# Narrower last key tile and first score block, a shorter inverse square root, and a final scaling in quarters

## The chip, the cores and the metric

The kernel runs on one core of one Trainium2 chip. The metric is the device time of one execution in microseconds (us), the median of several runs. Engines go by the names of the profile: PE is TensorE (PEld its weight loads), DVE is VectorE, ACT is ScalarE, POOL is GpSimd, SP is the engine that issues most DMAs.

## What is computed

One layer on 1024 tokens of width 1024, in float32: an RMS norm, one input projection, latent attention with 16 heads, a gated output projection added to x, then a second gated product (the embedding part, called PLE), and a final RMS norm. What matters here is the attention of one query block of 128 tokens, which sees only the keys up to its own end:

```python
for blk in range(S // Q_BLOCK):          # 8 blocks of 128 queries
    q0, q1 = blk * Q_BLOCK, (blk + 1) * Q_BLOCK
    s = (q_nope[q0:q1] @ k_nope[:q1].T + q_rope[q0:q1] @ k_rope[:q1].T) * scale
    s = where(k_chunk <= q_chunk, s, -inf)      # chunks of 64 tokens
    outs.append(softmax(s) @ v[:, :q1])
...
return rmsnorm(x, final_norm)            # x * (mean(x*x) + eps) ** -0.5 * gain
```

## The kernel before

Every matrix operand is split into a high part and the rest (`hi`, `lo`, both of type float32r), and a product is made of three matmuls, hi by hi, hi by lo and lo by hi. Each matmul of the program comes with a load of its own stationary operand of 128x128.

The work goes in stages: the projection of the norms (`u_tile`, with L215 and L216), the gate path (L513), the attention over 16 heads, the output projection and the PLE product (both in `product`, L751).

In the attention, `blocks` (L683) lists 16 heads times 8 query blocks, in the order 5, 4, 2, 3, 7, 6, 0, 1 within a head (the last head has its own order). One loop (L685) runs over them with an offset for each step: `scores` for block n, `prob_transposes` for block n-2, `values` for block n-4. The projections of later heads are put between them (L690 to L706). That program order is PE's order.

- `scores` (L598) multiplies one query block with its keys, three matmuls for each span of columns. Block 0 has 128 keys; its span is 256 columns wide (L604), of which `s` (L611) uses the first 128. The masking, the maximum and the exponential follow on DVE and ACT.
- `prob_transposes` (L641) transposes the probabilities tile by tile on PE into a PSUM tile; ACT copies them out as `hi` (L650) and DVE subtracts to get `lo` (L651). Two query blocks of a pair g = i // 2 share one tile: the even block is in columns 0 to 127, the odd one in columns 128 to 255.
- `values` (L653) multiplies the values with the pair's probabilities, 2g + 2 key tiles, a `hi` and a `lo` matmul for each, 256 columns wide. The even block does not see the last key tile, so its half of that tile is zero; four memsets (L537 to L539) set these zeros once.

At the end, each token tile goes through the PLE product, a sigmoid, two elementwise operations and a sum of squares; `rsqrt` (L93) makes the inverse root on DVE with an integer estimate and three Newton steps, and the tile is scaled and stored (L838 to L845). For the last tile, POOL has multiplied columns 0 to 511 with the gain beforehand (L836), and ACT scales them while DVE scales and multiplies the others. The two halves are then stored by two DMAs from SP. `rsqrt` is also called for the norms of `u_tile` (two columns), once for eight columns (L381), and for each of the 16 tiles of the two last stages (one column).

Of the kernel before, what the change touches and what calls it, by code (L numbers as in the profile page):

```python
# [9 lines left out]
F32 = mybir.dt.float32  # L10
F32R = mybir.dt.float32r
BF16 = mybir.dt.bfloat16
I32 = mybir.dt.int32
AF = mybir.ActivationFunctionType
ALU = mybir.AluOpType
AX = mybir.AxisListType

P = 128
S = 1024
D = 1024  # L20
# [31 lines left out]
def mla_ple_kernel(ctx, tc, x, x_t, p_t, pos, norm_g, w_c, w_z, q_norm, w_q, w_r, kv_norm, w_k, w_v,  # L52
# [6 lines left out]
    nc = tc.nc  # L59
    V, A, G = nc.vector, nc.scalar, nc.gpsimd  # L60

    def pool(name, bufs=1, **kw):
        return tc.tile_pool(name=name, bufs=bufs, **kw)
# [3 lines left out]
    def ps_big():  # L67
        return psum.tile([P, 1024], F32, tag="big", name="ps_big", bufs=2)

    def ps_tr():  # L70
        return psum.tile([P, 512], F32, tag="one", name="ps_tr", bufs=4)

    def ps_o():
        return psum.tile([P, 512], F32, tag="one", name="ps_o", bufs=4)

    def ps_pj():
        return psum.tile([P, 512], F32, tag="one", name="ps_pj", bufs=4)
# [10 lines left out]
    small = ctx.enter_context(pool("small", bufs=4))  # L88
# [3 lines left out]

    def rsqrt(v, n, name="rs_y", bufs=None):  # L93

        half = small.tile([P, n], I32, tag=f"rs_i{n}", name="rs_i", bufs=2)
        V.tensor_scalar(out=half, in0=v.bitcast(I32), scalar1=1, scalar2=None,
                        op0=ALU.logical_shift_right)
        y = small.tile([P, n], F32, tag=f"{name}{n}", name=name, bufs=bufs)
        V.tensor_scalar(out=y.bitcast(I32), in0=half, scalar1=-1, scalar2=0x5F3759DF,
                        op0=ALU.mult, op1=ALU.add)  # L100
        t = small.tile([P, n], F32, tag=f"rs_t{n}", name="rs_t", bufs=2)
        if n == 1:
            h = small.tile([P, 1], F32, tag="rs_h", name="rs_h", bufs=2)
            V.tensor_scalar(out=h, in0=v, scalar1=-0.5, scalar2=None, op0=ALU.mult)
            for _ in range(3):
                V.tensor_scalar(out=t, in0=y, scalar1=y, scalar2=h, op0=ALU.mult, op1=ALU.mult)
                V.scalar_tensor_tensor(out=y, in0=t, scalar=1.5, in1=y, op0=ALU.add, op1=ALU.mult)
            return y
        for _ in range(3):
            V.scalar_tensor_tensor(out=t, in0=y, scalar=-0.5, in1=y, op0=ALU.mult, op1=ALU.mult)  # L110
            V.tensor_tensor(out=t, in0=t, in1=v, op=ALU.mult)
            V.scalar_tensor_tensor(out=y, in0=t, scalar=1.5, in1=y, op0=ALU.add, op1=ALU.mult)
        return y
# [37 lines left out]
    ps = ps_tr()  # L151
# [232 lines left out]
    for t in range(NT):  # L384
        V.tensor_scalar(out=krw[:, t, :], in0=krw[:, t, :], scalar1=rx[:, t:t + 1], scalar2=None,
                        op0=ALU.mult)
# [116 lines left out]
    for c in range(KT):  # L503
        ps = ps_big()
        for k in range(KT):
            if k % 4 == 0:
                n = 2 * c + k // 4
# [3 lines left out]
            for a, b in pairs:  # L511
                for hf in range(2):
                    nc.tensor.matmul(ps[:, hf * 512:(hf + 1) * 512], wz[b][:, k % 4, :],  # L513
                                     (hT_hi, hT_lo)[a][:, k, hf * 512:(hf + 1) * 512],
                                     start=k == 0 and a + b == 0, stop=k == KT - 1 and a == 1)
# [18 lines left out]


    pt_w = [[att.tile([P, n, 2 * P], F32R, name=f"pt{n}{z}") for z in "hl"] for n in (4, 8)]
    for n, w in zip((4, 8), pt_w):  # L537
        for z in w:
            G.memset(z[:, n - 1, :P].bitcast(F32), 0.0)  # L539
    pt = [[z[:, (2, 0, 2, 0)[g]:, :] for z in pt_w[g // 2]] for g in range(4)]  # L540
    vals = att.tile([P, NT, 2, 4, VD], F32R, name="vals")
    kst = att.tile([P, S], F32, name="kst")

    def prob_tile():
        return att.tile([P, S], F32, tag="prob", name="prob", bufs=3)
# [49 lines left out]
    def order(h):  # L595
        return LAST if h == H - 1 else ORDER

    def scores(h, i):  # L598
        e = h % 2
        q = q_of[h]  # L600
        qs = slice(i * P, (i + 1) * P)
        n = (i + 1) * P
        off = P if n == 640 else 0
        spans = {128: [(0, 256)], 640: [(0, 384), (384, 640)]}.get(  # L604
            n, [(a, min(a + 512, n)) for a in range(0, n, 512)])
        ps = ps_big() if n > P else ps_tr()
        for s0, s1 in spans:
            for a, b in pairs:
                nc.tensor.matmul(ps[:, off + s0:off + s1], q[a][:, qs], (k_hi, k_lo)[b][e][:, s0:s1],  # L609
                                 start=a + b == 0, stop=a == 1)  # L610
        s = ps[:, off:off + n]  # L611
        V.memset(s[0:64, n - 64:], MASKED)
        mx = small.tile([P, 1], F32, tag="mx", name="mx")
        V.tensor_reduce(out=mx, in_=s, axis=AX.X, op=ALU.max, negate=True)  # L614
        pr = prob_tile()
        if e == 0 and i == order(h)[0]:
            sums[h // 2] = small.tile([P, 2 * NT], F32, tag="l", name="l", bufs=2)
        l = sums[h // 2][:, e * NT + i:e * NT + i + 1]
        A.activation(out=pr[:, :n], in_=s, func=AF.Exp, bias=mx, scale=1.0, accum_out=l)  # L619
        return pr  # L620
# [32 lines left out]
    def values(h, g):  # L653
        e, c = h % 2, h // 2
        hi, lo = pt[g]
        ps = ps_o()
        last = 2 * g + 1
        for j in range(last + 1):
            w = vals[:, j, c % 2, 2 * e:2 * e + 2, :]
            for n, z in enumerate((hi, lo)):  # L660
                nc.tensor.matmul(ps[:, :256], w, z[:, j, :], start=j + n == 0, stop=j == last and n == 1)  # L661
        top, bot = slice(e * VD, (e + 1) * VD), slice((1 - e) * VD, (2 - e) * VD)
        o = att.tile([P, 256], F32, tag="o1", name="o1", bufs=2)
        A.copy(out=o[top], in_=ps[bot, :256])
        V.tensor_tensor(out=o[top], in0=ps[top, :256], in1=o[top], op=ALU.add)  # L665
        z = zT[top, c, g * 256:(g + 1) * 256]
        (V if h >= H - 2 else G).tensor_tensor(out=z, in0=o[top], in1=z, op=ALU.mult)  # L667
# [17 lines left out]
    for n in range(len(blocks) + LAGV):  # L685
        if n < len(blocks):
            h, i = blocks[n]
# [21 lines left out]
        if n >= LAGV and (blocks[n - LAGV][1] ^ 1) in order(blocks[n - LAGV][0])[:(n - LAGV) % NT]:  # L709
            h, i = blocks[n - LAGV]  # L710
# [34 lines left out]
    halves = (slice(0, 512), slice(512, D))  # L745

    def product(ps, st, w, nk, spans):
        for k in range(nk):
            for a, b in pairs:
                for o, cols in zip(ps, spans):  # L750
                    nc.tensor.matmul(o, st[a][:, k, :], w[k][b][:, cols],  # L751
                                     start=k == 0 and a + b == 0, stop=k == nk - 1 and a == 1)
# [9 lines left out]
    xs = fin.tile([P, NT, D], F32, name="xs")  # L762
# [26 lines left out]
    for t in range(NT):  # L789
# [4 lines left out]
        ps = ps_big()  # L794
# [17 lines left out]
    for t in range(NT):  # L812
        (gl, pl), nxt = nxt, gate_lhs(t + 1) if t + 1 < NT else None
        ps = ps_big()
        last = t == NT - 1
        edges = (0, 512, 768, D) if last else (0, 512, D)
        spans = [slice(*z) for z in zip(edges, edges[1:])]
        pp = [ps_pj()[:, :z.stop - z.start] for z in spans]
        ms = small.tile([P, 3], F32, tag="ms2", name="ms2", bufs=2)
        for i, cols in enumerate(spans):  # L820
            n = cols.stop - cols.start
            po = ps_tr()[:, :n] if i == 2 else ps[:, cols]
            product([po], gl, w_g, KT, [cols])
            if i != 1:
                product(pp[i:i + 2], pl, w_p, PLE // P, spans[i:i + 2])
            sg = fin.tile([P, 512], F32, tag="sg", name="sg", bufs=2)[:, :n]
            A.activation(out=sg, in_=po, func=AF.Sigmoid, scale=r2[t])
            V.tensor_tensor(out=sg, in0=pp[i], in1=sg, op=ALU.mult)
            V.tensor_tensor(out=xs[:, t, cols], in0=xs[:, t, cols], in1=sg, op=ALU.add)  # L829
            jk = fin.tile([P, D], BF16, tag="jk", name="jk", bufs=1)  # L830
            mean_square(ms[:, i:i + 1], xs[:, t, cols], D, jk[:, :n])
            if i:
                V.scalar_tensor_tensor(out=ms[:, i:i + 1], in0=ms[:, i - 1:i], scalar=EPS if i == 1 else 0.0,
                                       in1=ms[:, i:i + 1], op0=ALU.add, op1=ALU.add)
            elif last:
                G.tensor_tensor(out=xs[:, t, cols], in0=xs[:, t, cols], in1=f_bc[:, cols], op=ALU.mult)  # L836
        r = rsqrt(ms[:, i:i + 1], 1, name="r3", bufs=2)
        for hf in range(2):  # L838
            cols = halves[hf]
            if last and hf == 0:  # L840
                A.activation(out=xs[:, t, cols], in_=xs[:, t, cols], func=AF.Copy, scale=r)
            else:
                V.scalar_tensor_tensor(out=xs[:, t, cols], in0=xs[:, t, cols], scalar=r,
                                       in1=f_bc[:, cols], op0=ALU.mult, op1=ALU.mult)
            nc.sync.dma_start(out=out[t * P:(t + 1) * P, cols], in_=xs[:, t, cols])  # L845


# [48 lines left out]
```

## Time and profile before

| | |
|---|---|
| median of 3 runs | 719.05 us (718.22 to 720.75) |
| profiled execution | 719.65 us, span 717.9 us |
| PE busy | 703.2 us (98%), 4032 matmuls |
| PEld busy | 612.9 us (85%), 4032 loads |
| DVE busy | 523.8 us (73%) |
| ACT busy | 400.5 us (56%) |
| POOL busy | 214.2 us (30%) |
| TensorE clock granted | full in nearly all of the span (mean 0.998) |

The span is the stretch that the profile covers; the execution's own time is 1.75 us more. Matmuls are pipelined and their ends are modelled, so a busy PE is not a PE at its peak: what one matmul costs in a dense stream is the distance from its start to the next start, not its duration.

### The profile page before, as it was taken

Reading aid. Unit: us, or ns where it says so; the run is one execution under the profiler, and the core shown is the slowest. Engines: PE = TensorE matmul, PEld = TensorE weight load, DVE = VectorE, ACT = ScalarE, POOL = GpSimd, SP = SyncE. Lnnn points to the kernel's source line nnn. Section 1 sums busy time; section 2 is a strip of 40 time slices with the busy share of each in tenths; the row PEclk is TensorE's granted clock in tenths of the full one; section 3 lists DMA queues with packets and bytes.
Section 4 is the critical chain, followed back from the end, with each engine's and each line's share of the span. In section 5 each row is a group of like instructions: output and inputs, shape, how many; then the busy total and the mean of one; then the engine's idle time right before and its main releaser. Section 6 shows DMA issues by size and latency. Waiting matters only on the chain.

```text
span 717.9 us, 11582 instructions
## 1 busy us (share of the span) xinstructions
PE 703.2 (98%) x4032; PEld 612.9 (85%) x4032; DVE 523.8 (73%) x1298; ACT 400.5 (56%) x920; POOL 214.2 (30%) x236
## 2 busy tenths in 40 slices
PE   9999999999999999999999999989999999999995
PEld 7999888888988899889988899878878888888884
DVE  6995553417888888888888888899564168888754
ACT  6752343417777767877767787776353145342322
POOL 0000443214145434554335532264155142000000
PEclk9999999999999999999999999999999999999999
DMA  8720334314103402052211421032573030111101
GB/s 318 279 89 12 122 100 125 103 60 110 38 16 108 147 31 74 1 181 74 66 40 60 136 60 60 15 108 85 179 265 115 1 102 24 38 37 37 60 30 59
DMA packets 26907, 63.95 MB, mean 89 GB/s; under 512 B 4568, under 2 KB 8544, under 8 KB 26848
## 3 DMA queue, kind: packets, MB, share of 16 engines
q1 hardware_dynamic: 23168, 52.19, 22.8%
q0 software_dynamic: 3536, 11.02, 4.6%
q8 instruction: 32, 0.52, 0.3%
q14 instruction: 27, 0.22, 0.1%
q10 hardware_dynamic: 144, 0.00, 0.0%
HBM read 50.01 MB, written 13.18 MB: 88 GB/s over the span
## 4 chain that ended last, share of the span: by engine, by line
PE 90%; DVE 3%; ACT 3%; DMA 2%; issue 1%; POOL 0%; SPq 0%; ACTq 0%; DVEq 0%
PE ps_big L751 21%; PE ps_big L609 13%; PE ps_big L513 12%; PE ps_o L661 10%; PE ps_tr L121 9%; PE ps_pj L423 6%; PE ps_big L215 4%; PE ps_pj L751 3%; PE ps_pj L570 3%; PE ps_pj L553 3%; PE ps_big L216 3%; PE ps_o L215 1%; PE ps_pj L216 1%; DMA wst<-in_w_out 1%; ACT prob L619 1%; PE ps_tr L609 1%
## 5 line engine op out<-in xcount | busy, mean ns | idle before, releaser
L751 PE MATMUL ps_big<-w,aTh 128*128 128x512 f32 (+1 forms) x480 | 139.0, 390 | 0.0
L751 PEld LDWEIGHTS ps_big<-w,aTh 128*128 128x128 f32 x480 | 89.4, 188 | 20.2
L619 ACT ACTIVATE prob<-ps_big,mx 128x384 f32<-128x384 f32 (+6 forms) x112 | 89.4, 798 | 16.2 <-DVE mx L614 15.5
L614 DVE TENSOR_REDUCE mx<-ps_big 128x1 f32<-128x384 f32 (+6 forms) x112 | 91.6, 818 | 1.8
L121 PE MATMUL ps_tr<-ident,prob 128*128 128x128 f32 x576 | 84.1, 273 | 2.0 <-ACT prob L619 2.0
L751 PE MATMUL ps_big<-w,aTl 128*128 128x512 f32 (+1 forms) x240 | 84.6, 390 | 0.0
L121 PEld LDWEIGHTS ps_tr<-ident,prob 128*128 128x128 f32 x576 | 68.3, 140 | 11.7 <-ACT prob L619 2.8
L91 DVE TENSOR_TENSOR pt8l<-ps_tr,pt8h 128x512 fp32r<-128x512 f32 (+3 forms) x128 | 71.0, 582 | 4.5 <-ACT pt8h L650 3.8
L667 POOL TENSOR_TENSOR zT<-o,zT 64x256 f32<-64x256 f32 x56 | 41.1, 736 | 94.2 <-DVE o L665 80.6
L609 PE MATMUL ps_big<-k_hi,qh 128*128 128x512 f32 (+2 forms) x176 | 67.7, 385 | 0.9 <-ACT prob L619 0.8
L650 ACT CAST pt8h<-ps_tr 128x512 fp32r<-128x512 f32 (+3 forms) x128 | 60.7, 509 | 4.7 <-PE ps_tr L121 4.3
L609 PE MATMUL ps_big<-k_lo,qh 128*128 128x512 f32 (+2 forms) x176 | 62.0, 352 | 0.0
L609 PE MATMUL ps_big<-k_hi,ql 128*128 128x512 f32 (+2 forms) x176 | 61.4, 349 | 0.0
L661 PE MATMUL ps_o<-pt8h,vals 128*128 128x256 f32 x224 | 57.6, 294 | 0.0
L661 PE MATMUL ps_o<-pt8l,vals 128*128 128x256 f32 x224 | 55.0, 282 | 0.0
L751 PEld LDWEIGHTS ps_big<-w,aTl 128*128 128x128 f32 x240 | 45.0, 188 | 10.2 <-POOL aTl L91 0.5
L116 ACT ACTIVATE jk<-xs 128x512 bf16<-128x512 f32 (+2 forms) x25 | 18.8, 751 | 45.2 <-DVE xs L829 37.3
L661 PEld LDWEIGHTS ps_o<-pt8l,vals 128*128 128x128 f32 x224 | 42.9, 191 | 0.0
L661 PEld LDWEIGHTS ps_o<-pt8h,vals 128*128 128x128 f32 x224 | 42.6, 190 | 0.0
L650 ACT CAST pt4h<-ps_tr 128x384 fp32r<-128x384 f32 (+3 forms) x64 | 27.2, 426 | 27.3 <-PE ps_tr L121 27.1
L360 ACT ACTIVATE zh<-zs,g_col 128x128 fp32r<-128x128 f32 x56 | 18.3, 392 | 42.1 <-DMA zs<-in_w_z 36.1
L609 PEld LDWEIGHTS ps_big<-k_hi,qh 128*128 128x128 f32 x176 | 33.2, 189 | 7.7 <-ACT prob L619 3.5
(285 smaller groups left out, 1740.2 us busy)
## 6 DMA issues: line engine op xcount, KB each, us to landing
zT<-in_x SPq DMA_DIRECT2D x8, 512.0 KB, 5.0
rlb<-rl SPq DMA_DIRECT2D x32, 128.0 KB, 3.1
wst<-in_w_out SPq DMA_DIRECT2D x8, 512.0 KB, 4.4
xs<-in_x SPq DMA_DIRECT2D x8, 512.0 KB, 7.2
wst<-in_ple_gate SPq DMA_DIRECT2D x8, 512.0 KB, 4.0
out<-xs SPq DMA_DIRECT2D x16, 256.0 KB, 2.0
zs<-in_w_z SPq DMA_DIRECT2D x14, 256.0 KB, 2.9
zT<-in_x_t SPq DMA_DIRECT2D x6, 512.0 KB, 4.1
```

The costliest lines, as they stand in the source:

```text
L91: eng.tensor_tensor(out=lo, in0=src, in1=hi.bitcast(F32), op=ALU.subtract)
L121: nc.tensor.transpose(dst[:, j * P:(j + 1) * P], src[:, j * P:(j + 1) * P], ident)
L215: nc.tensor.matmul(pq, st, mv[:, k, :QL], start=first, stop=last)
L423: nc.tensor.matmul(ps, w[b][:, k, :], (cq_hi, cq_lo)[a][:, k, hf * 512:hf * 512 + 512], start=k == 0 and a + b == 0, stop=k == n - 1 and a ...
L513: nc.tensor.matmul(ps[:, hf * 512:(hf + 1) * 512], wz[b][:, k % 4, :], (hT_hi, hT_lo)[a][:, k, hf * 512:(hf + 1) * 512], start=k == 0 and ...
L609: nc.tensor.matmul(ps[:, off + s0:off + s1], q[a][:, qs], (k_hi, k_lo)[b][e][:, s0:s1], start=a + b == 0, stop=a == 1)
L614: V.tensor_reduce(out=mx, in_=s, axis=AX.X, op=ALU.max, negate=True)
L619: A.activation(out=pr[:, :n], in_=s, func=AF.Exp, bias=mx, scale=1.0, accum_out=l)
L650: A.copy(out=hi[:, j0:j0 + n, half], in_=src)
L661: nc.tensor.matmul(ps[:, :256], w, z[:, j, :], start=j + n == 0, stop=j == last and n == 1)
L667: (V if h >= H - 2 else G).tensor_tensor(out=z, in0=o[top], in1=z, op=ALU.mult)
L751: nc.tensor.matmul(o, st[a][:, k, :], w[k][b][:, cols], start=k == 0 and a + b == 0, stop=k == nk - 1 and a == 1)
```

## The change

The four memsets of zeros go. In `values`, the matmuls of the last key tile take columns 128 to 255 only, and the `lo` matmul of tile 0, which covers all columns, is moved from second place to the end, since it carries the stop mark. In `scores`, the special case for block 0 goes, so its span is 128 columns. In `rsqrt`, the shift and the multiplication by -1 become one multiplication of the integer by -0.5, and in the one-column form the first operation of a step is a scalar_tensor_tensor in place of a tensor_scalar with two per-partition scalars. For the last token tile, the scaling and storing goes by four quarters of 256 columns instead of two halves, the first two on ACT, the others on DVE; the second quarter's DMA is issued by ACT, the other three by SP.

```diff
     def rsqrt(v, n, name="rs_y", bufs=None):
-        half = small.tile([P, n], I32, tag=f"rs_i{n}", name="rs_i", bufs=2)
-        V.tensor_scalar(out=half, in0=v.bitcast(I32), scalar1=1, scalar2=None,
-                        op0=ALU.logical_shift_right)
         y = small.tile([P, n], F32, tag=f"{name}{n}", name=name, bufs=bufs)
-        V.tensor_scalar(out=y.bitcast(I32), in0=half, scalar1=-1, scalar2=0x5F3759DF,
+        V.tensor_scalar(out=y.bitcast(I32), in0=v.bitcast(I32), scalar1=-0.5, scalar2=0x5F3759DF,
                         op0=ALU.mult, op1=ALU.add)
...
-                V.tensor_scalar(out=t, in0=y, scalar1=y, scalar2=h, op0=ALU.mult, op1=ALU.mult)
+                V.scalar_tensor_tensor(out=t, in0=y, scalar=y, in1=h, op0=ALU.mult, op1=ALU.mult)
...
-    for n, w in zip((4, 8), pt_w):
-        for z in w:
-            G.memset(z[:, n - 1, :P].bitcast(F32), 0.0)
...
-        spans = {128: [(0, 256)], 640: [(0, 384), (384, 640)]}.get(
+        spans = {640: [(0, 384), (384, 640)]}.get(
...
-        for j in range(last + 1):
-            w = vals[:, j, c % 2, 2 * e:2 * e + 2, :]
-            for n, z in enumerate((hi, lo)):
-                nc.tensor.matmul(ps[:, :256], w, z[:, j, :], start=j + n == 0, stop=j == last and n == 1)
+        steps = [(j, n) for j in range(last + 1) for n in range(2)]
+        steps.append(steps.pop(1))
+        for j, n in steps:
+            cols = slice(P if j == last else 0, 2 * P)
+            nc.tensor.matmul(ps[:, cols], vals[:, j, c % 2, 2 * e:2 * e + 2, :], (hi, lo)[n][:, j, cols],
+                             start=j + n == 0, stop=(j, n) == (0, 1))
...
-        for hf in range(2):
-            cols = halves[hf]
-            if last and hf == 0:
+        for i, cols in enumerate([slice(z, z + 256) for z in range(0, D, 256)] if last else halves):
+            on_act = last and i < 2
+            if on_act:
...
-            nc.sync.dma_start(out=out[t * P:(t + 1) * P, cols], in_=xs[:, t, cols])
+            (nc.scalar if on_act and i else nc.sync).dma_start(out=out[t * P:(t + 1) * P, cols], in_=xs[:, t, cols])
```

## Rows read from the trace of the kernel before

**Rows 1.** Windows, attention: busy us (count) PE, PEld, DVE, ACT, POOL; clock, DMA share, GB/s.

```profile
180.00:480.00 300.00, 299.63 (x2014) 271.07 (x2012) 258.39 (x555) 226.32 (x540) 125.31 (x130) 1.00 0.23 71
```

**Rows 2.** The page's chain that ended last: shares by engine, then by line.

```profile
PE 90%; DVE 3%; ACT 3%; DMA 2%; issue 1%; POOL 0%; SPq 0%; ACTq 0%; DVEq 0%
PE ps_big L751 21%; PE ps_big L609 13%; PE ps_big L513 12%; PE ps_o L661 10%; PE ps_tr L121 9%; PE ps_pj L423 6%; PE ps_big L215 4%; PE ps_pj L751 3%; PE ps_pj L570 3%; PE ps_pj L553 3%; PE ps_big L216 3%; PE ps_o L215 1%; PE ps_pj L216 1%; DMA wst<-in_w_out 1%; ACT prob L619 1%; PE ps_tr L609 1%
```

**Rows 3.** Groups by line and shape, PE: count | busy us, mean ns | idle before.

```profile
L661 PE MATMUL ps_o<-pt8l,vals 128*128 128x256 f32 x224 | 55.0, 282 | 0.0
L661 PE MATMUL ps_o<-pt4l,vals 128*128 128x256 f32 x96 | 24.4, 283 | 0.2 <-DVE pt4l L91 0.2
L609 PE MATMUL ps_tr<-k_hi,qh 128*128 128x256 f32 x16 | 4.5, 284 | 0.0
```

**Rows 4.** Timeline of PE in the attention: start us, duration us, instruction.

```profile
402.02 0.40 PE L553 MATMUL ps_pj<-ckv_hi,wkh 128*128 128x512 f32 x1
402.25 0.39 PE L553 MATMUL ps_pj<-ckv_hi,wkl 128*128 128x512 f32 x1
...
403.35 0.28 PE L609 MATMUL ps_big<-k_hi,qh 128*128 128x256 f32 x1
403.47 0.28 PE L609 MATMUL ps_big<-k_lo,qh 128*128 128x256 f32 x1
...
404.41 0.28 PE L661 MATMUL ps_o<-pt8h,vals 128*128 128x256 f32 x1
404.53 0.28 PE L661 MATMUL ps_o<-pt8l,vals 128*128 128x256 f32 x1
...
406.37 0.82 PE L121 MATMUL ps_tr<-ident,prob 128*128 128x128 f32 x6
```

**Rows 5.** Timeline of PEld in the same place.

```profile
404.41 0.19 PEld L661 LDWEIGHTS ps_o<-pt8l,vals 128*128 128x128 f32 x1
```

**Rows 6.** Timeline of the span's end, all engines.

```profile
711.15 0.15 DVE L96 TENSOR_SCALAR rs_i<-ms 128x1 int32<-128x1 int32 x1
711.22 0.14 DVE L104 TENSOR_SCALAR rs_h<-ms 128x1 f32<-128x1 f32 x1
711.34 0.15 DVE L99 TENSOR_SCALAR r<-rs_i 128x1 int32<-128x1 int32 x1
711.53 0.27 DVE L106 TENSOR_SCALAR rs_t<-r,rs_h 128x1 f32<-128x1 f32 x1
711.83 0.16 DVE L107 SCALAR_TENSOR_TENSOR r<-rs_t,r 128x1 f32<-128x1 f32 x1
...
713.04 0.75 DVE L843 SCALAR_TENSOR_TENSOR xs<-xs,r,f_bc 128x512 f32<-128x512 f32 x1
713.10 0.72 ACT L841 ACTIVATE xs<-xs,r 128x512 f32<-128x512 f32 x1 [2.17 <-DVE r L107]
713.84 0.81 SPq L845 DMA_DIRECT2D out<-xs  x2
```

**Rows 7.** Groups by line and shape, DVE.

```profile
L829 DVE TENSOR_TENSOR xs<-xs,sg 128x512 f32<-128x512 f32 x15 | 10.2, 683 | 0.1
L227 DVE TENSOR_SCALAR ms<-ms,eps 128x2 f32<-128x2 f32 x8 | 1.8, 226 | 6.9 <-ACT zT L116 6.9
L99 DVE TENSOR_SCALAR rs_y<-rs_i 128x2 int32<-128x2 int32 x8 | 1.3, 165 | 0.1
L829 DVE TENSOR_TENSOR xs<-xs,sg 128x256 f32<-128x256 f32 x2 | 0.8, 424 | 0.1
```

**Rows 8.** Groups by line and shape, ACT.

```profile
L827 ACT ACTIVATE sg<-ps_big,r 128x256 f32<-128x256 f32 x1 | 0.5, 474 | 0.7 <-PE ps_big L751 0.7
```

**Rows 9.** Windows at the span's end, columns as in rows 1.

```profile
714.50:715.00 0.50, 0.00 (x0) 0.00 (x0) 0.00 (x0) 0.00 (x0) 0.00 (x0) 0.50 0.65 238
715.50:716.00 0.50, 0.00 (x0) 0.00 (x0) 0.00 (x0) 0.00 (x0) 0.00 (x0) 0.50 1.03 389
716.00:716.50 0.50, 0.00 (x0) 0.00 (x0) 0.00 (x0) 0.00 (x0) 0.00 (x0) 0.50 0.12 41
```

**Rows 10.** Line 107 by itself: count, duration ns min/median/max, first and last start us.

```profile
L107 DVE SCALAR_TENSOR_TENSOR r<-rs_t,r x48: 159/160/2449, 531.7 to 712.8; 128x1 f32<-128x1 f32 x48
```

## The prediction, made before the result was known

> **What bounds the kernel now.** I read the page's chain of waits first [rows 2]: nine tenths of what ended last is PE, and PE's share is spread over all products; line 661 (the values) is 10% of it. Then the windows of the attention [rows 1]: of 300 us between 180 and 480, PE is busy 299.6, at the full clock, while DVE is busy 258 and ACT 226. So PE's own stream of instructions sets the time there, and an instruction of PE that gets shorter by some nanoseconds shortens the kernel by as much, as long as DVE (86% of the stretch) keeps up. Last comes the timeline of the end [rows 6]: from 711.1 on nothing but a chain of tiny DVE operations, a scaling and two stores is left, so each of them counts in full.
>
> Since a matmul's duration is pipelined and modelled, I price it by start to start [rows 4]: 402.02 to 402.25 is 0.23 us for 512 columns, 403.35 to 403.47 and 404.41 to 404.53 are 0.12 for 256. The narrowest in the trace is the transpose, 128 columns with a load of its own: six in a row last 0.82 with the last one's 0.27, so (0.82 - 0.27) / 5 = 0.11 each.
>
> **The change, part by part.** Narrower matmuls: `values` runs 16 heads x 4 pairs, two matmuls of the last tile each, so 128 are narrowed; they belong to the 640 of line 661, of which the `lo` halves are 224 + 96 [rows 3]. `scores` of block 0 adds 3 x 16 = 48 (three groups of 16, one shown [rows 3]). Together 176, at 0.12 us now: 21.1 us of PE.
>
> What does one cost at 128 columns? No row shows a float32r matmul under 256 columns, so it has to be bounded. By the streaming alone, 256 columns less are worth 0.23 - 0.12 = 0.11 us, so 128 less are worth 0.055, and the slot would be 0.065. [...] From above, if a narrow matmul was streamed several times over, the nearest row is the 512-column one, four times 128 columns: 0.23. I take the row of the same width and with the same kind of load, the transpose: 0.11. Against 0.12 this is 0.01 each, 176 x 0.01 = 1.8 us saved. The ends I keep are 176 x 0.055 = 9.7 saved and 176 x 0.11 = 19.4 lost.
>
> The Trainium skill bears on this (TensorE: Matmul & The Clock Gate, section LDWEIGHTS): a weight load takes its columns over 1.2 GHz, 107 ns for 128 columns, and does not care how wide the moving operand is. The transposes' 0.11 agrees with it, and it speaks against a large gain, since every matmul here has its own load. The same page (section Back-to-back issue gap) gives 81 ns for a pair of load and matmul at 128 columns, by which 176 x 0.039 = 6.9 us would go, as an estimate from that page; but for 512 columns it gives 131 ns, where this trace has 230, so I do not lean on it.
>
> The order within `values`: the `lo` matmul of tile 0 goes last instead of second. Its operand was ready for the second place, so it is ready later too, and every matmul brings its own load in either order: 0. At the other end the accumulation ends as before with PE's last instruction of the group, so ACT's copy and DVE's add start as before. The four memsets on POOL stand ahead of the attention, on an engine that is busy 125 of the 300 us [rows 1]: 0.
>
> `rsqrt` ahead of the end: in the early norms, in the output projection and in all PLE tiles but the last one, DVE's small operations are beside PE's matmuls, 0. One thing gets dearer there: an operation with two tensor inputs can be held for up to 2.45 us (line 107, median 0.16 [rows 10]), which the tensor_scalar of line 106 with its single tensor is not; there are now six such operations instead of three for each tile. It would cost up to 3 x 2.4 = 7 us of DVE's time in a tile where all are held. In front of PE stands only the emptying of one of two PSUM buffers, and one tile's matmuls are 48 x 0.23 = 11 us, so this stays hidden: 0, bounded by 1 us lost.
>
> `rsqrt` at the end [rows 6]: the shift (711.15) and the estimate that waits for it (711.34) become one operation, beside which the half (711.22) is computed. The first step now starts 0.19 after the second of two independent operations, as 711.53 stands 0.19 behind 711.34: 711.22 + 0.19 = 711.41, so 0.12 saved. Each step's first operation is 0.27 with two per-partition scalars. One such scalar adds 226 - 165 = 61 ns [rows 7], so a scalar_tensor_tensor with one should take 0.16 + 0.06 = 0.22: 3 x 0.05 = 0.15 saved (from 0, if the second tensor costs as much as the scalar, to 3 x 0.11 = 0.33). Together 0.27, between 0.12 and 0.45.
>
> The last scaling and stores: let s be the start of DVE's scaling, 713.04 now [rows 6]. Now both halves are done at s + 0.79, SP issues at s + 0.80 and again about 0.4 later (both issues together last 0.81), and data flows from about s + 1.6 to s + 3.0: the DMA share is 1.03 at 389 GB/s in full flow, and 0.65 in the half microsecond from 714.5 on, so it began near 714.68, 0.8 after the issue; 0.12 in that from 716.0 on, so it ended near 716.06 [rows 9]. In quarters: DVE's 256 columns cost 0.75 - (0.683 - 0.424) = 0.49 [rows 6, 7], ACT's 0.47 [rows 8]. The first quarter is done at s + 0.51, the third at s + 0.49, the second and fourth at about s + 0.9. SP issues the first at s + 0.54, the third at s + 0.95 and the fourth at s + 1.35; ACT issues the second at s + 0.92. With 0.8 from issue to flow and 128 KB at 389 GB/s = 0.34, the quarters flow from s + 1.34, s + 1.72, about s + 2.0 and s + 2.3 on, the last until about s + 2.65. That is 0.4 less. From both sides: 0.1 lost (the fourth issue comes 0.15 after the second of now, and if a store's latency did not depend on its size, that is about all) to 0.6 saved.
>
> The sum: 1.8 + 0.27 + 0.4 = 2.5 us. The profiled execution took 719.65, so it would take 717.15; its span is 717.9 and the 1.75 around it don't change. The median of the runs shown is 719.05, 0.6 below that execution, so I forecast 716.5. With 0.5 to 1.9 saved in the attention (the starts are rounded to 0.01, so a slot may be 0.003 off) and 0.2 to 1.0 saved at the end, this case lies between 716.1 and 718.4. What can be told from no change in this kernel is 0.3%, 2.2 us: the forecast stands just beyond that.
>
> **The rivals.** First, the load hides deeper than I think, and a narrow matmul costs by its columns, 0.065: 9.7 + 0.7 = 10.4 saved, 708.6. For it: the slots at 512 and 256 go by columns with hardly a constant. Against it: the transposes' 0.11. DVE would then be busy 258 of 291 us, which still fits.
>
> Second, the slower side: narrow float32r matmuls lose their single pass. It sits at lines 609 (block 0) and 661 (last tile): if a matmul of 128 columns is streamed four times, it costs as the 512-column row, 0.23, and 176 x 0.11 = 19.4 us are lost on an engine without slack, less 0.7 at the end: 737.7. From two passes on (0.12, as now) the gain is gone; it decides for slower from three. The Trainium skill (FP8 and Floating Point Precision, section TensorE Precision Notes) has both kinds for 4-byte operands, a reduced one that reads them once and a full one of four passes; it states no width at which one becomes the other, and no run here shows one. For it: no float32r matmul under 256 columns occurs in the trace, so it excludes nothing. Against it: from 512 to 256 columns the cost per column does not rise, and the 128-column transposes need 0.11, not 0.23.
>
> Third, the change does not do what it says: the load at float32r takes the whole 0.12 (the load's record is 0.19 long [rows 5]), nothing goes in the attention, and only the end is left: 718.4.
>
> **How the numbers follow.** Forecast 62%, deeper hiding 12%, four passes 18%, nothing in the attention 8%. Faster by over 0.3% (under 716.9): the deeper hiding, and a little over half of the forecast's own range, 0.12 + 0.34 = 46%. Slower: 18%. The rest, 36%, is within 0.3%. The range leaves out the four passes alone: from 708.0, which takes in the first rival, to 719.8, which takes in the third with the end's loss. The likeliest case's own range stands above.
>
> **What would show it.** In the changed trace the start-to-start distance of the last tile's matmuls and of block 0's scores: 0.11 by the forecast, 0.065 and 0.23 by the rivals, 0.12 by the third. At the end, from the sum of squares to the scaling, 1.62 us instead of 1.89 (711.15 to 713.04), with a step's first operation at 0.22; and the last data 2.65 instead of 3.0 us after the scaling's start. The prediction is wrong if the distance is not near 0.11, or if PE gets idle time before `values` that the reordering brings.

## The result, and the profile after

The changed kernel takes 727.53 us (median of 4 runs, 725.27 to 728.76) against 719.63 for the kernel before (4 runs, 718.22 to 720.75): the ratio is 1.0107, with an interval of 1.0075 to 1.0139. It is slower by 7.9 us, where 2.5 us less were forecast. The profiled execution took 727.07, its span is 725.2. In the changed kernel the scores are line 603 (609 before), their exponential 613 (619), the transposes 118 (121), the values 656 (661), `product` 747 (751) and the end's scaling 839 (843).

The window of the attention comes first, with the columns of [rows 1].

```profile
180.00:480.00 300.00, 294.16 (x1966) 263.95 (x1965) 253.81 (x540) 221.40 (x524) 118.94 (x126) 1.00 0.23 68
```

PE was busy 299.63 of these 300 us [rows 1]; now it is idle for 5.8 of them, at the same clock, and 48 matmuls fewer start in them. Every other engine is less busy too, so none has become a bound by its load: PE waits for something. For what, PE's waits in this window say (line, releaser: total us, times, longest), first of the kernel after, then of the kernel before:

```profile
PE ps_big L603 <- ACT prob L613: 3.0, 6, 0.7
PE ps_o L656 <- DVE pt8l L91: 2.1, 3, 0.7
```

```profile
PE ps_big L609 <- ACT prob L619: 0.3, 1, 0.3
```

That is 5.1 of the 5.8 idle us, against a single wait of 0.3. The scores wait for an exponential to release their PSUM buffer (the tile that they are written to), the values for the `lo` probabilities. The page's chain, whose answer before is [rows 2], shows the same:

```profile
PE 75%; DVE 9%; ACT 9%; DMA 3%; issue 2%; POOL 2%; SPq 0%; ACTq 0%; DVEq 0%; POOLq 0%
```

PE's share fell from 90% to 75%; DVE and ACT rose from 3% to 9% each. PE's waits over the whole span, first of the kernel after:

```profile
PE ps_big L603 <- ACT prob L613: 3.9, 8, 0.7
...
PE ps_big L747 <- ACT sg L823: 1.1, 1, 1.1
```

and the same view of the kernel before:

```profile
PE ps_tr L121 <- ACT prob L619: 2.0, 2, 1.1
...
PE ps_o L661 <- DVE pt8l L91: 0.9, 1, 0.9
PE ps_big L609 <- ACT prob L619: 0.8, 2, 0.5
```

The scores, which waited 2 times, now wait 8 times, and the values 3 times instead of once. The transposes' two waits of before, 2.0 together, stand outside the window, and the kernel after does not have them.

**One place, in both traces.** The chain of waits of the kernel after, around the longest of these (start, us, what):

```profile
253.09 0.59 ACT qh L586
...
253.71 0.69 DVE ql L91
...
254.44 0.56 DVE pt8l L91
...
255.61 0.29 DVE pt4l L91
255.90 0.88 DVE mx L608
...
256.86 0.42 ACT prob L613
...
257.90 0.80 PE ps_big L603 x3
```

PE's timeline there ends its values and waits:

```profile
256.78 0.44 PE L656 MATMUL ps_o<-pt8l,vals 128*128 128x128 f32 x2
...
257.90 0.45 PE L603 MATMUL ps_big<-k_hi,qh 128*128 128x384 f32 x1 [0.68 <-ACT prob L613]
```

and DVE's has the start of the maximum, which the chain counts from the end of the operation before it:

```profile
255.82 0.95 DVE L608 TENSOR_REDUCE mx<-ps_big 128x1 f32<-128x768 f32 x1
```

Before, the same work stands in another order. First DVE's timeline, then ACT's, then PE's:

```profile
251.65 0.56 DVE L91 TENSOR_TENSOR pt8l<-ps_tr,pt8h 128x384 fp32r<-128x384 f32 x1 [0.16 <-ACT pt8h L650]
252.26 0.69 DVE L91 TENSOR_TENSOR ql<-ps_pj,qh 64x512 fp32r<-64x512 f32 x1
...
253.66 0.95 DVE L614 TENSOR_REDUCE mx<-ps_big 128x1 f32<-128x768 f32 x1
```

```profile
251.14 0.47 ACT L650 CAST pt8h<-ps_tr 128x384 fp32r<-128x384 f32 x1
251.64 0.58 ACT L592 CAST qh<-ps_pj 64x512 fp32r<-64x512 f32 x1
...
254.70 0.90 ACT L619 ACTIVATE prob<-ps_big,mx 128x768 f32<-128x768 f32 x1 [0.74 <-DVE mx L614]
```

```profile
252.19 0.42 PE L609 MATMUL ps_big<-k_hi,qh 128*128 128x384 f32 x1
...
255.54 0.28 PE L570 MATMUL ps_pj<-wvh,ckv_lo 128*128 128x256 f32 x1
255.75 0.44 PE L609 MATMUL ps_big<-k_hi,qh 128*128 128x384 f32 x1
```

Two things differ. ACT and DVE did the probabilities (`pt8h`, `pt8l`) ahead of the query split (`qh`, `ql`); now the split comes first, and DVE's maximum (`mx`) starts 1.83 us after the scores that stand at 252.19 before and at 253.99 after, instead of 1.47. And before, three matmuls of line 570 (a later head's values) stood between the values and the next scores and covered that delay; now they come behind the scores. None of this is in the diff, which touches none of these lines. The source gives the order only to begin with: when the kernel is built, a scheduler lays out each engine's stream. With only the two products changed (their widths, and the `lo` matmul moved), the built program has another instruction than before's in 197 places of PE's stream, 114 of ACT's and 146 of DVE's, and also in 15 of SP's and 4 of POOL's.

**Where the 7.3 us of span lie**, by starts read from the traces (one execution each, us, counted from PE's first matmul, 1.23 after the span's start). Single executions scatter by 1 to 2 us in the attention: e1 has before's PE order there and took 2.2 less.

| kernel | to first scores | to last values | to last matmul | to the end |
|---|---|---|---|---|
| before | 168.29 | 337.95 | 201.59 | 8.77 |
| after | 168.53 | 343.42 | 203.54 | 8.45 |
| e1 | 168.39 | 335.74 | 201.40 | 8.45 |
| e2 | 168.73 | 337.94 | 201.87 | 8.78 |
| e3 | 168.56 | 345.16 | 202.16 | 8.78 |
| e4 | 168.71 | 337.49 | 201.35 | 8.45 |
| e5 | 168.87 | 341.31 | 203.70 | 8.78 |
| e6 | 168.43 | 341.14 | 202.89 | 8.77 |
| e7 | 168.35 | 342.52 | 202.06 | 8.78 |
| e8 | 168.32 | 338.83 | 203.18 | 8.78 |

So the loss is 0.24 ahead of the attention, 5.5 in it and 1.95 behind it; the end gives 0.32 back. Of the 1.95, 1.1 is the wait for a sigmoid in the list above (`sg`, at 614.00), which the kernel before does not have.

**The narrow matmuls**, PE's timeline of the kernel after, answering [rows 4]: the end of a `values` group, then the next scores.

```profile
252.56 0.22 PE L656 MATMUL ps_o<-pt4h,vals 128*128 128x128 f32 x1
252.62 0.45 PE L656 MATMUL ps_o<-pt4l,vals 128*128 128x128 f32 x2
252.91 0.39 PE L603 MATMUL ps_big<-k_hi,qh 128*128 128x512 f32 x1
```

The row at 252.62 holds two matmuls, the narrow `lo` one and the moved one of tile 0, 256 wide. The narrow `hi` one is followed after 0.06, which looks like the 0.065 of a rival; but the three together, 252.56 to 252.91, take 0.35, against 3 x 0.12 before [rows 4]. Unrounded starts give 61, 115 and 170 ns: what the first distance lacks, the 256-wide matmul's distance has over (170 instead of 120). So a narrow matmul costs (346 - 120) / 2 = 113 ns.

**The end**, all engines, answering [rows 6]:

```profile
718.81 0.15 DVE L96 TENSOR_SCALAR r<-ms 128x1 int32<-128x1 int32 x1
...
719.06 0.22 DVE L103 SCALAR_TENSOR_TENSOR rs_t<-r,rs_h 128x1 f32<-128x1 f32 x1
...
720.41 0.88 DVE L839 SCALAR_TENSOR_TENSOR xs<-xs,r,f_bc 128x256 f32<-128x256 f32 x2
...
720.92 1.30 SPq L841 DMA_DIRECT2D out<-xs  x3
721.40 0.35 ACTq L841 DMA_DIRECT2D out<-xs  x1
```

and the windows of the four stores, answering [rows 9] (the last two columns are the share of the DMA engines and GB/s):

```profile
721.50:722.00 0.50, 0.00 (x0) 0.00 (x0) 0.00 (x0) 0.00 (x0) 0.00 (x0) 0.50 0.48 158
722.00:722.50 0.50, 0.00 (x0) 0.00 (x0) 0.00 (x0) 0.00 (x0) 0.00 (x0) 0.50 0.84 266
722.50:723.00 0.50, 0.00 (x0) 0.00 (x0) 0.00 (x0) 0.00 (x0) 0.00 (x0) 0.50 1.03 340
723.00:723.50 0.50, 0.00 (x0) 0.00 (x0) 0.00 (x0) 0.00 (x0) 0.00 (x0) 0.50 0.86 285
```

From the first dependent operation to the scaling it is 1.60 (718.81 to 720.41) instead of 1.89. The last data, by the last window's share of 0.86 against 1.03 in full flow, ended near 723.42 (723.0 + 0.5 x 0.86 / 1.03), 3.0 behind the scaling's start, as before.

### The profile page after: what moved, and what is told of

It is laid out like the page before. It is cut to its first block, busy times and chain, and to the rows that moved or that the text cites. A ratio compares the mean times of both kernels' runs of the same rounds, so it can differ in the third digit from the quotient of the medians.

```text
span 725.2 us, 11549 instructions
## 1 busy us (share of the span) xinstructions
PE 704.9 (97%) x4032; PEld 611.9 (84%) x4032; DVE 516.4 (71%) x1274; ACT 402.7 (56%) x921; POOL 213.9 (29%) x232
## 4 chain that ended last, share of the span: by engine, by line
PE 75%; DVE 9%; ACT 9%; DMA 3%; issue 2%; POOL 2%; SPq 0%; ACTq 0%; DVEq 0%; POOLq 0%
PE ps_big L747 21%; PE ps_big L510 12%; PE ps_big L603 9%; PE ps_o L656 6%; PE ps_tr L118 6%; PE ps_pj L420 5%; PE ps_big L212 3%; ACT prob L613 3%; PE ps_pj L547 3%; PE ps_pj L747 3%; PE ps_big L213 3%; DVE mx L608 2%; PE ps_pj L564 2%; DVE pt8l L91 2%; DMA rlb<-rl 1%
## 5 line engine op out<-in xcount | busy, mean ns | idle before, releaser
L644 ACT CAST pt8h<-ps_tr 128x512 fp32r<-128x512 f32 (+3 forms) x128 | 59.0, 509 | 6.4 <-PE ps_tr L118 5.8
L656 PE MATMUL ps_o<-pt8h,vals 128*128 128x256 f32 x224 | 51.9, 286 | 0.0
L656 PE MATMUL ps_o<-pt8l,vals 128*128 128x256 f32 (+1 forms) x224 | 50.6, 289 | 0.0
L656 PEld LDWEIGHTS ps_o<-pt8h,vals 128*128 128x128 f32 x224 | 40.1, 190 | 0.2 <-DVE pt8l L91 0.2
L656 PEld LDWEIGHTS ps_o<-pt8l,vals 128*128 128x128 f32 x224 | 40.1, 190 | 0.0
L644 ACT CAST pt4h<-ps_tr 128x384 fp32r<-128x384 f32 (+3 forms) x64 | 26.7, 425 | 19.7 <-PE ps_tr L118 19.4
```

The source lines that it names most:

```text
L644: A.copy(out=hi[:, j0:j0 + n, half], in_=src)
L656: nc.tensor.matmul(ps[:, cols], vals[:, j, c % 2, 2 * e:2 * e + 2, :], (hi, lo)[n][:, j, cols], start=j + n == 0, stop=(j, n) == (0, 1))
```

## The experiments

Theory: the narrow matmuls and the end each save a little, and the order of the engines' streams, which changes with the widths, costs more than both. The rivals: the narrow matmuls themselves are dearer than they look, or the end's edits disturb what stands ahead of them. To tell them apart, each engine's order can be held when the kernel is built: behind the traced program, every instruction is made to follow the one that stood before it in another kernel's order. It adds an order, no work (`runs_of` is the other kernel's order, `order` that of one engine):

```diff
+def hold_order(tc, runs_of):
...
+    info = mybir.DependencyInfo(mybir.DependencyClass.NoSync, mybir.DependencyReason.DATA)
...
+        for a, b in zip(order, order[1:]):
+            tc.add_manual_dep(ins[b], ins[a].name, info, reason="hold")
```

The four memsets are kept in every experiment; leaving them out changes no place in the built order of PE, ACT, DVE and SP. e1 to e4 share their 25 runs of the kernel before (719.89), e5 to e8 theirs (7 runs, 719.38). Differences in us are the ratio times that median.

**e1: the end alone**, `rsqrt` and the quarters.

```diff
...
-                V.tensor_scalar(out=t, in0=y, scalar1=y, scalar2=h, op0=ALU.mult, op1=ALU.mult)
+                V.scalar_tensor_tensor(out=t, in0=y, scalar=y, in1=h, op0=ALU.mult, op1=ALU.mult)
...
-        for hf in range(2):
+        for i, cols in enumerate([slice(z, z + 256) for z in range(0, D, 256)] if last else halves):
```

> The kernel before with only the shorter inverse root and the last tile's scaling in quarters; no matmul is narrowed and PE's order is that of before. Order theory (the loss comes from the order in which the scheduler puts the attention's instructions once some matmuls are narrow): nothing of the loss is here, 0.7 us faster than before. Rival (the extra two-tensor operations of the inverse root are held behind POOL and delay PE): 1 to 7 us slower than before.

Measured: 719.19 (12 runs), ratio 0.9986 (0.9975 to 0.9997). Faster by 1.0 us, with an interval of 0.2 to 1.8; its trace has the last stretch 0.32 shorter, as in the kernel after. PE's order is before's. The end's edits cause none of the loss.

**e2: narrow matmuls, before's order** on every engine.

```diff
-        spans = {128: [(0, 256)], 640: [(0, 384), (384, 640)]}.get(
+        spans = {640: [(0, 384), (384, 640)]}.get(
...
+            cols = slice(P if j == last else 0, 2 * P)
...
+        hold_order(tc, RUNS)
```

> The kernel before with the 176 narrow matmuls and the moved lo matmul, every engine held to the order of the kernel before; the four memsets stay. Order theory: a narrow matmul takes a slot of 0.112 us instead of 0.119, 176 x 0.007 = 1.3 us faster than before. Rival (narrow matmuls, or accumulating into half of a PSUM tile, cost PE themselves): 7 to 9 us slower than before, as the changed kernel.

Measured: 719.0 (12 runs), ratio 0.9988 (0.9977 to 0.9998): 0.9 us saved, between 0.1 and 1.7. Four passes or more, which would cost 19.4, are excluded, and so is 0.065 a matmul, which would save 9.7.

**e3: the order alone.** The 256-wide matmuls of before, all their work kept, held to the order that the program gets with the narrow ones.

```diff
+        hold_order(tc, RUNS)
```

> The kernel before with all its 256-column matmuls, every engine held to the order that the scheduler gives the kernel with narrow matmuls. Order theory: the loss of the changed kernel (7.9 us) and what it saved (1.3 by narrow matmuls, 0.7 at the end), so about 9.5 us slower than before. Rival (cost of narrow matmuls themselves): as before, within 1 us.

Measured: 728.57 (4 runs), ratio 1.0119 (1.0105 to 1.0134). The order alone costs 8.6 us (7.6 to 9.6). At the place shown above its PE timeline has the same wait with wide matmuls:

```profile
257.29 0.28 PE L661 MATMUL ps_o<-pt8l,vals 128*128 128x256 f32 x1
258.20 0.44 PE L609 MATMUL ps_big<-k_hi,qh 128*128 128x384 f32 x1 [0.64 <-ACT prob L619]
```

and its list of PE's waits is nearer to that of the kernel after than to before's:

```profile
PE ps_big L609 <- ACT prob L619: 3.3, 6, 0.7
PE ps_o L661 <- DVE pt8l L91: 1.8, 3, 0.6
```

**e4: the whole change but the memsets, held to e1's order** (PE's is before's).

```diff
+        hold_order(tc, RUNS)
```

> The whole change (narrow matmuls, shorter root, quarters), held to the order that the kernel has with its end changed alone, which on PE is that of before; the four memsets stay. Order theory: the savings without the loss, 1.3 + 0.7 = 2.0 us faster than before, 10 us faster than the changed kernel. Rival (cost of the narrow matmuls themselves): 7 us slower than before.

Measured: 718.4 (7 runs), ratio 0.9974 (0.9963 to 0.9985), which is the product of e1's and e2's. This version beats both kernels, the one before by 0.26% and, over the two ratios (0.9974 / 1.0107), the one after by 1.3%. Its PE is free of the wait at that place; the values are followed by line 567, which was 570:

```profile
255.11 0.44 PE L659 MATMUL ps_o<-pt8l,vals 128*128 128x128 f32 x2
255.39 0.28 PE L567 MATMUL ps_pj<-wvh,ckv_hi 128*128 128x256 f32 x1
...
255.63 0.28 PE L567 MATMUL ps_pj<-wvh,ckv_lo 128*128 128x256 f32 x1
255.89 0.44 PE L606 MATMUL ps_big<-k_hi,qh 128*128 128x384 f32 x1
```

**e5 and e6: whose order costs.** Both have the narrow matmuls of e2. e5 holds PE alone to before's order, so that ACT (113 places) and DVE (156) differ from before; e6 holds ACT and DVE, so that PE differs in 138 places. SP's order differs from before's in 15 places in both, POOL's in 4 in e5.

```diff
 RUNS = {
     "PE": "0 17 57 3 17 4 ...",
-    "Activation": "1 1 0 1 2 11 ...",
-    "DVE": "0 2 3 1 2 1 ...",
```

> The 176 narrow matmuls with PE alone held to the order of the kernel before; ACT and DVE get the order that the scheduler chooses for narrow matmuls (113 and 156 of their places differ from before). If PE's own order makes the waits (scores ahead of the projections that used to fill the time): 1 us faster than before. If the order on ACT and DVE does (copies for a later projection ahead of the probabilities that PE needs): about 8 to 9 us slower than before.

> The narrow matmuls with ACT and DVE held to the order of the kernel before; PE's order is the scheduler's own (138 places differ from before). If PE's order makes the waits: 8 to 9 us slower than before. If the order on ACT and DVE does: 1 us faster than before, at most 2 us slower.

Measured: e5 724.66, ratio 1.008 (1.0064 to 1.0095); e6 722.84, ratio 1.0054 (1.0038 to 1.007), 4 runs each. That is neither of the two outcomes expected of each: it is not one engine's order alone. Against e2's 0.9 saved, the new order costs 5.8 + 0.9 = 6.7 us with PE held (e5) and 3.9 + 0.9 = 4.8 with ACT and DVE held (e6). The two are not parts of e3's 8.6, and need not sum to it: with the others held the scheduler chooses anew, and e6's PE order differs from e3's in 86 places. What SP's places do in them was not separated; but in e7 below SP's order is before's, and the loss is there. In e5's waits the scores alone account for most of it, 5.1 against 0.8 before:

```profile
PE ps_big L609 <- ACT prob L619: 5.1, 9, 1.0
```

**e7 and e8: which narrowing brings the order.** e7 narrows the last key tile of `values` only (128 matmuls, with the `lo` matmul moved), e8 block 0's scores only (48); nothing is held.

```diff
-                nc.tensor.matmul(ps[:, :256], w, z[:, j, :], start=j + n == 0, stop=j == last and n == 1)
+            cols = slice(P if j == last else 0, 2 * P)
```

```diff
-        spans = {128: [(0, 256)], 640: [(0, 384), (384, 640)]}.get(
+        spans = {640: [(0, 384), (384, 640)]}.get(
```

> Only the last key tile of the values is narrow (128 of the 176 matmuls), nothing held. Its order on ACT and DVE is nearly that of the changed kernel (6 and 14 places differ). Order theory: 8 to 9 us slower than before. Theory that the loss goes with the number of narrow matmuls: 128/176 of 9.5, less its saving, 6 us slower.

> Only the scores of block 0 are narrow (48 of the 176), nothing held; 147 places on PE, 54 on ACT and 95 on DVE differ from before. Order theory: slower than before by part of the loss, some 1 to 5 us, by the waits that its own order makes. Theory by number: 48/176 of 9.5, 2.6 us, less 0.4 saved.

Measured: e7 725.01, ratio 1.0084 (1.0068 to 1.0101); e8 722.05, ratio 1.0046 (1.0031 to 1.0061), 4 runs each. Each brings a dear order, and with what their narrow matmuls save taken in, they cost 6.0 and 3.3 us. For e7 the order theory had expected 8 to 9 and missed; 6 is what a loss that goes with the number of narrow matmuls would make. e7 and e8 alone don't refute that theory, but e3 and e2 do: with none narrow in the changed order the kernel loses 8.6, with all 176 narrow in the old order it loses nothing.

**e9: block 0's scores in two spans of 64 columns**, for the price of a narrow matmul at another width; one run.

```diff
-        spans = {128: [(0, 256)], 640: [(0, 384), (384, 640)]}.get(
+        spans = {128: [(0, 64), (64, 128)], 640: [(0, 384), (384, 640)]}.get(
```

> The scores of block 0 by two spans of 64 columns instead of one of 256 (six matmuls instead of three for each head), nothing else changed and nothing held. Read from the trace, block 0's group from its first start to the next matmul's true start. If the weight load sets the slot of a narrow matmul: 6 x 0.112 = 0.67 us for a group, whatever the 64 columns stream. If the columns do: 64 columns are 0.034 at the slope of 0.44 ns each, 6 x 0.034 = 0.2 us. If a narrow matmul lost its single pass: 6 x 0.12 = 0.72 us, but then 128 columns would have shown 0.23 each.

Measured: 729.49, against 721.27 before. The order has changed here too, so the time says little; the slots do. PE's timeline:

```profile
291.20 0.20 PE L609 MATMUL ps_tr<-k_hi,qh 128*128 128x64 f32 x1
291.24 0.28 PE L609 MATMUL ps_tr<-k_lo,qh 128*128 128x64 f32 x1
291.35 0.28 PE L609 MATMUL ps_tr<-k_hi,ql 128*128 128x64 f32 x1
...
291.68 0.28 PE L609 MATMUL ps_tr<-k_hi,ql 128*128 128x64 f32 x1
291.79 0.48 PE L423 MATMUL ps_pj<-cq_hi,wqh 128*128 128x512 f32 x1
292.11 0.40 PE L423 MATMUL ps_pj<-cq_hi,wql 128*128 128x512 f32 x1
```

At 64 columns the distance is 0.11, as at 128; the first is 0.04, and the 512-wide one behind them takes 0.32 instead of 0.23. From 291.20 to 292.11 are 0.91; less 0.23 and over six it is 0.113 each. Between 64 and 128 columns the width does not set the price, and 256 columns cost hardly more (0.12).

## Why the prediction was wrong

**The step that failed** stands under the whole sum: that the stream each engine executes stays as it was, but for the moved `lo` matmul, so that a change of the order is not a term of the sum ("At the other end the accumulation ends as before with PE's last instruction of the group, so ACT's copy and DVE's add start as before"), with the order of the source as PE's order. It is not, even in the kernel before: the list of its PE stream in e5's cut above (first instruction in the source's order, how many) goes from the 17 that start at 0 to three that start at 57. The range priced only durations, and the order fell out of it: e3 puts it at 8.6 us, e2 puts all narrowing with the order kept at -0.9. With e1's -1.0 the sum is 6.7; measured are 7.7 by the ratio, between 5.4 and 10.0. The slower rival named the wrong mechanism (four passes): a narrow matmul is not dear, by e2 and by the slots. The sentence on PE idle "before `values` that the reordering brings" comes nearest, but meant the moved matmul, and the longer waits are before the scores.

What was left out can be read from the rows of before: an engine that is busy 299.63 of 300 us [rows 1], fed by two engines at 75 and 86%, has hardly a wait only because each buffer comes free in time. That is a property of one particular order, and the matmul starts show how tight it is: at 255.75 the scores started 0.09 later than a slot of 0.12 behind 255.54 allows, and the exponential that frees their buffer, at 254.70 with 0.90, had ended only at 255.60. Another order of the streams turns such near misses into waits, as e3 shows.

**Point by point.**

- Slot of a narrow matmul: forecast 0.11 instead of 0.12, right (113 ns against 120). The saving was over-sized, since its 0.01 is the difference of two rounded starts: 64 groups x (360 - 346) = 0.9 and, for the scores, 48 matmuls at 8 ns = 0.4, together 1.3 instead of 1.8, and e2 measured 0.9 (0.1 to 1.7). The prediction read the cost per column as not rising from 512 to 256 columns; its slots of 0.23 and 0.12 are 0.45 and 0.47 ns a column, a small rise.
- The Trainium skill (TensorE: Matmul & The Clock Gate, section LDWEIGHTS) has a load's time go by its own columns alone, over 1.2 GHz, which makes 107 ns of 128, an estimate from that page. e9's equal price at 64 and 128 columns agrees with it, at 113. The same page's 81 ns for a pair at 128 columns (section Back-to-back issue gap) does not hold for these matmuls: over a run they stand 113 apart. That the load sets this price is argued from the equal prices; no run changed the load.
- The memsets' going and the moved matmul, both at 0: neither was run by itself. In e2, where the `lo` matmul is moved and the order held, nothing is lost. But with all widths kept, moving it alone gives the built program another order too, in 20 places of PE's stream and 2 each of ACT's and DVE's; what those cost is open.
- `rsqrt` in the earlier stages, cost at nothing though operations with two tensors can be held: right. The rows of the new step operation in e1 (ns, smallest, median, largest) show that it is held like line 107 [rows 10], while e1's stretch behind the attention is no longer than before's (201.40 against 201.59).

```profile
L103 DVE SCALAR_TENSOR_TENSOR rs_t<-r,rs_h x48: 219/220/2337, 529.3 to 710.0; 128x1 f32<-128x1 f32 x48
```

- `rsqrt` at the end: forecast 0.27 saved, 0.29 measured; a step's first operation 0.22, as forecast from one per-partition scalar's 61 ns.
- The quarters: forecast 0.4 saved, measured 0. The flow began at 1.36 behind the scaling's start, close to the forecast 1.34; the term's mistake is the rate. Four stores with half as wide a row flow at 340 GB/s in the fullest window, the two halves at 389 [rows 9], and the window before that one is at a share of 0.84 instead of 1.03; why was not tried. What starts earlier flows longer, and ends at the same 3.0. The forecast's own sum was short as well: from its 1.72 on, three quarters of 0.34 end at 2.74, not 2.65, which is 0.3 saved and not 0.4.
- The end in all: 0.32 by the trace, against 0.67 forecast; e1's median has 1.0 (0.2 to 1.8), which does not contradict either.

**What stays open.** Why the scheduler lays out the streams differently for a narrow matmul was not tried on the chip; the runs show only that it comes, and what it costs; in e8, where nothing but a width changes, PE's stream differs from before's in 147 places, ACT's in 54 and DVE's in 95. Of the 1.95 us behind the attention, the wait for the sigmoid is in the traces of after, e5 (0.8), e6 (0.4) and e8 (0.3), not in those of e3 and e7; which instruction's place decides it was not separated.

## What to carry to other kernels

Where a scheduler lays out the engines' streams, a change of an instruction's size can also be a change of order: compare the orders of the two kernels before any duration, and price a near-full engine's waits for its neighbours as a term of its own. Hold the old order and run the change, then run the old work in the new order: two kernels part the two effects, and here the first is the version to keep. And here a matmul with its own 128-column weight load gained next to nothing below 256 columns (113 ns against 120).

## What the runs showed of the hardware

A narrow matmul's recorded starts mislead: the first of a run is followed after 0.04 (64 columns) or 0.06 (128), and the first wider one behind them takes 0.05 to 0.09 more than its slot. Only the distance over the whole run, to the start behind the first wide matmul, gives the price: 0.113 at 64 and at 128 columns. A tile stored in quarters of 1 KB a partition flowed at 340 GB/s at a DMA share of 1.03, in halves of 2 KB at 389 at the same share, each in one window of half a microsecond.
